# Delta-rule blocks: key transposes and key/query products issued one hook step later

## The chip, the cores and the metric

One core of a Trainium2 chip runs the whole program. The metric is the device time of one execution in microseconds (us); lower is better. In what follows TensorE does the matmuls and transposes (PE in the rows, PEld for its weight loads), VectorE is DVE, ScalarE is ACT, GpSimd is POOL, and SyncE (SP) issues nearly all DMAs.

## What is computed

One decoder layer over 2048 tokens of width 1024: an RMS norm, one combined input projection, two token mixers in parallel, a gated merge and an output projection. All of it is float32. Mixer A is a chunked gated delta rule with 4 heads of width 128 and a short causal convolution ahead of it; mixer B is dilated sliding-window attention. The part that matters here is the preparation of mixer A:

```python
qkv = jax.nn.silu(causal_depthwise_conv(dn_qkv, conv_w[layer]))      # width 4
dq, dk, dv = jnp.split(qkv.astype(jnp.float32), 3, axis=-1)
dq = l2_normalize(to_heads(dq)) * (HEAD_DIM ** -0.5)
dk = l2_normalize(to_heads(dk))
...
decay = jnp.exp(jnp.where(causal, gc[..., :, None] - gc[..., None, :], -jnp.inf))
lower = jnp.where(strict, jnp.einsum('bhnid,bhnjd->bhnij', kb, k) * decay, 0.0)
a_intra = jnp.where(causal, jnp.einsum('bhnid,bhnjd->bhnij', q, k) * decay, 0.0)
```

For every head the keys have to be convolved, gated, transposed and normed, and the products of keys with keys and of keys with queries have to be formed and multiplied with a decay matrix. Norms and signs are applied later as scales of rows.

## The kernel before, in words

The program has stages: attention (mixer B) with its projections; then the "channel units", in which TensorE multiplies 128 columns of the input weight with the normed input; inside them, as background work, the delta-rule preparation, an inverse and a scan; at the end the output. The change lies among the channel units.

`cunits` runs over the units. A unit has four blocks of 512 tokens (n = 0 to 3). A block is 24 matmuls into one accumulator `mm` (three buffers): for each of eight k, three products of high and low parts (L524 to L526). After every second k, thus after two groups of three matmuls, `hook()` is called; a block has four such hook steps, the last of them after its last matmul. When a block is done, the unit's own function is called with the accumulator, and it queues its later steps by `self.at(d, f)`: f is called in the d-th hook after that. The order in which the Python code issues instructions in this part is the order in which TensorE, VectorE, ScalarE and GpSimd execute them, since it is pinned for these four engines; the DMAs of SP are ordered by the scheduler. Steps that fall due in one hook are called by their tick and then by the length that the list of waiting steps had when they were queued.

For each of the four heads there is a unit of keys (`k_block`), one of queries (`q_block`) and one of values (`v_block`), twelve units in a row. All three start with `conv`: ScalarE evicts the accumulator into `xr` (L624), VectorE (or for values ScalarE, L630) scales it into `acc` (L628) and adds three shifted products (L632). Four hooks later the gate follows: tanh on ScalarE (L636) and a product on VectorE (L637), which gives `kT` or `qT`.

- Keys: `pe(0)` and `pe(2)` each transpose two 128x128 pieces of kT on TensorE into a buffer `tp` (L688; two buffers), and ScalarE reads each piece twice, for the sum of squares (L692) and scaled into `kd` (L693). `fin` makes the norms on GpSimd (L700 to L706).
- Queries: `prep(0)` and `prep(2)` split keys and queries into high and low parts, ScalarE writing `kqh` (L727) and GpSimd `kql` (L728; two buffers each). `pe(0)` and `pe(2)` transpose two pieces of qT (L737), form the products by three matmuls for each of two pieces (L741 to L743) into `sc`, ScalarE takes squares (L745) and VectorE multiplies with the decay matrix E (L746), which `pe(2)` then stores with four DMAs. `fin` makes the norms (L760 to L762).
- Values: `pe` transposes four pieces seven hooks after the block (L780, read by L783).

`e_chain` makes the decay matrices of a head, four blocks one after the other through a single buffer `gcb`: a DMA loads it (L651), GpSimd adds the causal mask (L655), VectorE makes four differences (L662) and ScalarE their exponentials (L669). For the first head it starts ahead of the first key unit, for each later head in the value unit of the head before. The weights of the next unit are loaded and split in the same steps (ScalarE L78, GpSimd L79).

Of the kernel before, what the change touches and what calls it, by code (L numbers as in the profile page):

```python
# [36 lines left out]
def dr(ap, off, dims):  # L37
    return bass.AP(tensor=ap.tensor, offset=ap.offset + off, ap=[list(d) for d in dims])


class Net:
# [634 lines left out]
    def k_block(self, h, n, pr):  # L676
        nc, dp = self.nc, self.dp
        if n == 0:
            self.kT = dp.tile([P, T], F32, name="kT", bufs=1)
        kT = self.kT[:, n * 512:(n + 1) * 512]  # L680
        self.conv(n, 4 + h, pr, kT, lambda: self.recput(n, h, R_KT, P, kT.rearrange("p (a c) -> p a c", c=P)))
        ss = dp.tile([P, 12], F32, name="ss", bufs=3)
        kd = dp.tile([P, 4, P], F32, name="st4", bufs=2)

        def pe(t0):
            pt = self.ps.tile([P, 512], F32, name="tp", bufs=2)
            for t in (t0, t0 + 1):
                nc.tensor.transpose(pt[:, (t - t0) * P:(t - t0 + 1) * P], kT[:, t * P:(t + 1) * P], self.ident)  # L688
            for t in (t0, t0 + 1):
                c = h * 16 + n * 4 + t  # L690
                a = pt[:, (t - t0) * P:(t - t0 + 1) * P]
                nc.scalar.activation(kd[:, t, :], a, AF.Square, accum_out=ss[:, t:t + 1])  # L692
                nc.scalar.activation(kd[:, t, :], a, AF.Identity, scale=self.ek[:, c:c + 1])  # L693
            if t0 == 2:
                self.recput(n, h, R_KD, P, kd)

        def fin():
            cs = slice(h * 16 + n * 4, h * 16 + n * 4 + 4)
            G = nc.gpsimd
            G.tensor_scalar(out=ss[:, 0:4], in0=ss[:, 0:4], scalar1=4 * EPS, scalar2=None, op0=ALU.add)  # L700
            G.tensor_tensor(out=ss[:, 4:8], in0=ss[:, 0:4], in1=self.mhalf[:, 0:4], op=ALU.pow)
            G.tensor_tensor(out=ss[:, 8:12], in0=ss[:, 4:8], in1=self.beta[:, cs], op=ALU.mult)
            G.tensor_scalar(out=self.vss[:, cs], in0=ss[:, 8:12], scalar1=0.5, scalar2=None, op0=ALU.mult)
            G.tensor_tensor(out=ss[:, 8:12], in0=ss[:, 8:12], in1=ss[:, 4:8], op=ALU.mult)
            G.tensor_scalar(out=self.nbr[:, cs], in0=ss[:, 8:12], scalar1=-1.0, scalar2=None, op0=ALU.mult)
            G.tensor_tensor(out=self.ksn[:, cs], in0=self.nbr[:, cs], in1=self.egc[:, cs], op=ALU.mult)  # L706
        self.at(7, lambda: pe(0))
        self.at(9, lambda: pe(2))
        self.at(11, fin)

    def q_block(self, h, n, pr):
        nc, dp = self.nc, self.dp
# [9 lines left out]
        def prep(t0):  # L722
            kqh = dp.tile([P, 2, 2, P], F32R, name="kqh", bufs=2)
            kql = dp.tile([P, 2, 2, P], F32R, name="kql", bufs=2)
            kq[t0] = kqh, kql
            for j, src in enumerate((kv, qv)):
                nc.scalar.activation(kqh[:, :, j, :], src[:, t0:t0 + 2, :], AF.Copy)  # L727
                nc.gpsimd.tensor_tensor(out=kql[:, :, j, :], in0=src[:, t0:t0 + 2, :], in1=kqh[:, :, j, :].bitcast(F32),  # L728
                                        op=ALU.subtract)

        def pe(t0):
            E = self.E[h, n]
            kqh, kql = kq[t0]
            pt = self.ps.tile([P, 512], F32, name="tp", bufs=2)
            pk = self.ps.tile([P, 512], F32, name="sc", bufs=2)
            for t in (t0, t0 + 1):
                nc.tensor.transpose(pt[:, (t - t0) * P:(t - t0 + 1) * P], qT[:, t * P:(t + 1) * P], self.ident)  # L737
            for j in (0, 1):
                b = pk[:, j * 256:j * 256 + 256]
                rh, rl = (a[:, j].rearrange("p a c -> p (a c)") for a in (kqh, kql))  # L740
                nc.tensor.matmul(b, kqh[:, j, 0, :], rh, start=True, stop=False)  # L741
                nc.tensor.matmul(b, kqh[:, j, 0, :], rl, start=False, stop=False)
                nc.tensor.matmul(b, kql[:, j, 0, :], rh, start=False, stop=True)  # L743
            for t in (t0, t0 + 1):
                nc.scalar.activation(sq, pt[:, (t - t0) * P:(t - t0 + 1) * P], AF.Square, accum_out=ss[:, t:t + 1])  # L745
            nc.vector.tensor_tensor(out=la[:, t0:t0 + 2], in0=pk.rearrange("p (a b c) -> p a b c", b=2, c=P),  # L746
                                    in1=E[:, t0:t0 + 2, :].unsqueeze(2).to_broadcast([P, 2, 2, P]),
                                    op=ALU.mult)
            if t0 == 2:
                lt = la[:, :, 0, :]  # L750
                self.recput(n, h, R_AT, P, la[:, :, 1, :])
                self.recput(n, h, R_LO, 64, lt[0:64, :, 64:128], 64)
                for s in (0, 1):
                    nc.sync.dma_start(dr(self.lscr, ((h * 16 + n * 4) * 2 + s) * 4096, [[64, 64], [8192, 4], [1, 64]]),
                                      lt[s * 64:(s + 1) * 64, :, s * 64:(s + 1) * 64])
# [6 lines left out]
            G.tensor_scalar(out=self.cq[:, cs], in0=ss[:, 4:8], scalar1=SCALE, scalar2=None, op0=ALU.mult)  # L762
        self.at(6, lambda: prep(0))
        self.at(7, lambda: prep(2))
        self.at(9, lambda: pe(0))
        self.at(10, lambda: pe(2))
        self.at(12, fin)

    def v_block(self, h, n, pr):
        nc, dp = self.nc, self.dp  # L770
# [446 lines left out]
```

## Time and profile before

| | |
|---|---|
| median of 3 runs | 2385.1 us (2384.5 to 2389.4) |
| the profiled execution | 2384.28 us |
| its span, first to last instruction | 2382.4 us |
| granted TensorE clock, mean | 0.996 |
| busy: TensorE / VectorE / ScalarE / GpSimd | 98% / 50% / 36% / 37% |
| the delta-rule units, four heads | about 1119 to 1441 us, some 80 us a head |

The profile is one execution. Busy shares are of the span. A row of the timeline gives the start, the length, the engine, the line, the operation, and in brackets the idle time ahead of it with what ended it. Starts are measured; the ends of matmuls are modelled, which is why a row of pipelined matmuls seems to overlap.

### The profile page before, as it was taken

The numbers are of one execution on the slowest core, as the hardware profiler recorded it, in microseconds if no ns is written. First come the engines' busy times: TensorE is split into PE (matmuls) and PEld (weight loads), VectorE is DVE, ScalarE is ACT, GpSimd is POOL, SyncE is SP. The second block draws the span as 40 slices with busy tenths as digits, with TensorE's granted clock in tenths as the row PEclk, the third lists the DMA queues.
The fourth block names the chain that finished last, engine by engine and source line by source line (L and its number), as shares of the span: only waits on it lengthen the run. The fifth ranks groups of instructions, "written<-read, shape, count | busy, mean of one in ns | idle before, by whom it ended". The sixth has DMA issues, their size and how long they took to land.

```text
span 2382.4 us, 40700 instructions
## 1 busy us (share of the span) xinstructions
PE 2343.1 (98%) x13640; PEld 2133.7 (90%) x13640; DVE 1191.4 (50%) x2831; ACT 847.5 (36%) x3021; POOL 886.0 (37%) x1855
## 2 busy tenths in 40 slices
PE   8999999999999999999999999999999999999999
PEld 7899999999999999988878888888888878889988
DVE  5543344334334434344877775999344433454431
ACT  6433333344444434333666662111233313111110
POOL 6633333333333334310855671101233212433441
PEclk9999999999999999999999999999999999999999
DMA  8443344333333335233544443222577645554542
GB/s 283 158 116 111 107 123 121 95 103 112 110 97 112 108 91 128 86 91 92 142 121 130 116 115 116 69 73 75 193 209 203 182 151 157 164 178 156 149 140 75
DMA packets 378808, 307.30 MB, mean 129 GB/s; under 512 B 61352, under 2 KB 345320, under 8 KB 378216
## 3 DMA queue, kind: packets, MB, share of 16 engines
q1 hardware_dynamic: 378312, 304.64, 43.6%
q8 instruction: 108, 1.77, 0.3%
q14 instruction: 100, 0.82, 0.1%
q10 hardware_dynamic: 288, 0.07, 0.0%
HBM read 187.92 MB, written 116.69 MB: 128 GB/s over the span
## 4 chain that ended last, share of the span: by engine, by line
PE 85%; POOL 4%; DMA 4%; DVE 4%; ACT 2%; issue 2%; SPq 0%; POOLq 0%; ACTq 0%; DVEq 0%
PE mm L240 10%; PE mm L238 10%; PE mm L239 10%; PE mm L524 9%; PE mm L526 9%; PE mm L525 9%; PE mm L1054 2%; PE mm L1052 2%; PE mm L1053 2%; PE mm L1035 2%; PE mm L1037 2%; PE mm L1036 2%; PE po L333 2%; PE tp L290 2%; DMA gcb<-gcscr 1%
## 5 line engine op out<-in xcount | busy, mean ns | idle before, releaser
L238 PE MATMUL mm<-wh,hh 128*128 128x384 f32 (+1 forms) x1536 | 555.0, 361 | 6.3 <-ACT hh L131 2.9
L240 PE MATMUL mm<-wh,hl 128*128 128x384 f32 (+1 forms) x1536 | 519.7, 338 | 1.7 <-DVE hl L135 1.7
L239 PE MATMUL mm<-wl,hh 128*128 128x384 f32 (+1 forms) x1536 | 518.3, 337 | 0.7 <-DVE wl L79 0.6
L524 PE MATMUL mm<-hh,wh 128*128 128x512 f32 x1152 | 464.1, 403 | 0.0
L526 PE MATMUL mm<-hh,wl 128*128 128x512 f32 x1152 | 454.7, 395 | 0.0
L525 PE MATMUL mm<-hl,wh 128*128 128x512 f32 x1152 | 451.4, 392 | 0.0
L238 PEld LDWEIGHTS mm<-wh,hh 128*128 128x128 f32 x1536 | 290.2, 189 | 10.8 <-ACT wh L78 4.4
L239 PEld LDWEIGHTS mm<-wl,hh 128*128 128x128 f32 x1536 | 291.0, 189 | 1.7 <-DVE wl L79 1.1
L240 PEld LDWEIGHTS mm<-wh,hl 128*128 128x128 f32 x1536 | 289.3, 188 | 2.6 <-DVE hl L135 2.6
L526 PEld LDWEIGHTS mm<-hh,wl 128*128 128x128 f32 x1152 | 217.0, 188 | 46.9
L525 PEld LDWEIGHTS mm<-hl,wh 128*128 128x128 f32 x1152 | 217.4, 189 | 41.8
L524 PEld LDWEIGHTS mm<-hh,wh 128*128 128x128 f32 x1152 | 217.2, 189 | 42.0
L263 DVE SCALAR_TENSOR_TENSOR rec<-mm,st,wqk 128x128 f32<-128x128 f32 x384 | 116.7, 346 | 263.7 <-POOL st L255 244.2
L79 POOL TENSOR_TENSOR wl<-raw,wh 128x512 fp32r<-128x512 f32 (+1 forms) x73 | 104.6, 1445 | 382.3 <-ACT wh L78 382.0
L317 ACT ACTIVATE p<-sc,ol 128x128 f32<-128x128 f32 (+1 forms) x192 | 82.1, 428 | 316.8 <-DVE ol L315 273.0
L253 POOL TENSOR_SCALAR st<-st 128x2 f32<-128x2 f32 x192 | 38.0, 198 | 399.7 <-ACT rec L249 398.2
L249 ACT ACTIVATE rec<-mm 128x128 f32<-128x128 f32 x384 | 102.7, 273 | 185.0 <-PE mm L240 171.8
L1035 PE MATMUL mm<-oh,hh 128*128 128x256 f32 x512 | 143.9, 281 | 2.9 <-DVE gt L1039 2.9
L1037 PE MATMUL mm<-oh,hl 128*128 128x256 f32 x512 | 142.9, 279 | 0.0
L1036 PE MATMUL mm<-ol,hh 128*128 128x256 f32 x512 | 142.9, 279 | 0.0
L255 POOL TENSOR_TENSOR st<-st,mhalf 128x2 f32<-128x2 f32 x192 | 135.0, 703 | 16.0
L632 DVE SCALAR_TENSOR_TENSOR acc<-xr,cw,acc 128x512 f32<-128x512 f32 x144 | 122.4, 850 | 17.4 <-ACT acc L630 12.4
(244 smaller groups left out, 4332.0 us busy)
## 6 DMA issues: line engine op xcount, KB each, us to landing
rscr<-rec SPq DMA_DIRECT2D x192, 192.0 KB, 1.9
raw<-in_w_in_dram SPq DMA_DIRECT2D x138, 256.0 KB, 3.1
qk<-rscr SPq DMA_DIRECT2D x192, 128.0 KB, 2.2
gscr<-gt SPq DMA_DIRECT2D x64, 256.0 KB, 2.4
gt<-gscr SPq DMA_DIRECT2D x64, 256.0 KB, 3.5
oscr<-ol SPq DMA_DIRECT2D x192, 65.0 KB, 2.0
oc<-oscr SPq DMA_DIRECT2D x16, 780.0 KB, 5.3
v<-rscr SPq DMA_DIRECT2D x192, 64.0 KB, 2.0
```

The lines of the kernel that those rows point to most:

```text
L238: nc.tensor.matmul(pr[:, :w], a, wh[:, k, :w], start=(k == 0), stop=False)
L239: nc.tensor.matmul(pr[:, :w], a, wl[:, k, :w], start=False, stop=False)
L240: nc.tensor.matmul(pr[:, :w], b, wh[:, k, :w], start=False, stop=(k == KT - 1))
L255: nc.gpsimd.tensor_tensor(out=st[:, 2:4], in0=st[:, 0:2], in1=self.mhalf[:, 0:2], op=ALU.pow)
L263: nc.vector.scalar_tensor_tensor(out=qk[:, j, :], in0=pr[:, j * P:(j + 1) * P], scalar=st[:, 2 + j:3 + j], in1=s["w"][2][:, j, :], op0=ALU ...
L524: nc.tensor.matmul(pr, wh[:, k, :], a, start=(k == 0), stop=False)
L525: nc.tensor.matmul(pr, wh[:, k, :], b, start=False, stop=False)
L526: nc.tensor.matmul(pr, wl[:, k, :], a, start=False, stop=(k == KT - 1))
L632: nc.vector.scalar_tensor_tensor(out=acc, in0=xr[:, j:j + 512], scalar=w[:, j:j + 1], in1=acc, op0=ALU.mult, op1=ALU.add)
L1035: nc.tensor.matmul(o, self.wbh[:, k, ms], oh[:, k, :], start=(k == b * 4), stop=False)
L1036: nc.tensor.matmul(o, self.wbh[:, k, ms], ol[:, k, :], start=False, stop=False)
L1037: nc.tensor.matmul(o, self.wbl[:, k, ms], oh[:, k, :], start=False, stop=(k == b * 4 + 3))
```

## The change

In `k_block` the two pairs of transposes and the step `fin` are queued for one hook later (7, 9, 11 become 8, 10, 12). In `q_block` the two groups of transposes and products and `fin` are queued one hook later too (9, 10, 12 become 10, 11, 13); `prep` stays at 6 and 7. Nothing else is changed, and no instruction is added or taken away.

```diff
 def k_block(self, h, n, pr):
...
-        self.at(7, lambda: pe(0))
-        self.at(9, lambda: pe(2))
-        self.at(11, fin)
+        self.at(8, lambda: pe(0))
+        self.at(10, lambda: pe(2))
+        self.at(12, fin)
...
 def q_block(self, h, n, pr):
...
         self.at(6, lambda: prep(0))
         self.at(7, lambda: prep(2))
-        self.at(9, lambda: pe(0))
-        self.at(10, lambda: pe(2))
-        self.at(12, fin)
+        self.at(10, lambda: pe(0))
+        self.at(11, lambda: pe(2))
+        self.at(13, fin)
```

On TensorE, in the second head's key unit, the first pair of key transposes before (mm_15320 is the accumulator of the unit's third block, mm_15371 of its fourth):

```order
L688 MATMUL tp_15343<-ident_69,kT_15243 128x128 x2
L524 MATMUL mm_15320<-hh_67,wh1_14955 128x512
L525 MATMUL mm_15320<-hl_68,wh1_14955 128x512
L526 MATMUL mm_15320<-hh_67,wl1_14956 128x512
...
L524 MATMUL mm_15371<-hh_67,wh1_14955 128x512
```

and after the change:

```order
L525 MATMUL mm_15320<-hl_68,wh1_14952 128x512
L526 MATMUL mm_15320<-hh_67,wl1_14953 128x512
L688 MATMUL tp_15352<-ident_69,kT_15243 128x128 x2
L524 MATMUL mm_15371<-hh_67,wh1_14952 128x512
L525 MATMUL mm_15371<-hl_68,wh1_14952 128x512
```

The pair stood before the last six matmuls of a block; now it stands between two blocks. On ScalarE, at the same pair, the order before (kT from acc is the tanh of the next block's gate, L78 the split of a weight, L624 an eviction):

```order
L669 ACTIVATE E_15300<-E_15300,nlc_13338 128x128 x4
L692 ACTIVATE st4_15253,ss_15252<-tp_15343 128x128
L693 ACTIVATE st4_15253<-tp_15343,ek_13340 128x128
...
L636 ACTIVATE kT_15243<-acc_15313 128x512
L78 ACTIVATE wh1_15254<-raw_15258 128x512
L624 ACTIVATE xr_15361<-mm_15320 128x512
```

and now:

```order
L669 ACTIVATE E_15300<-E_15300,nlc_13338 128x128 x4
L636 ACTIVATE kT_15243<-acc_15313 128x512
L692 ACTIVATE st4_15253,ss_15252<-tp_15352 128x128
L693 ACTIVATE st4_15253<-tp_15352,ek_13340 128x128
...
L78 ACTIVATE wh1_15254<-raw_15258 128x512
L624 ACTIVATE xr_15361<-mm_15320 128x512
```

The gate of the next block now precedes the four reads of the pair. On ScalarE in the second head's query unit, around the first block's two groups (sq are the squares of the queries, kqh the high parts for the second block), a piece of the difference:

```order
 L624 ACTIVATE xr_15621<-mm_15563 128x512
-L745 ACTIVATE sq_15491,ss_15490<-tp_15639 128x128 x2
-L745 ACTIVATE sq_15491,ss_15490<-tp_15658 128x128 x2
-L727 ACTIVATE kqh_15675<-kT_15243 128x2x128
-L727 ACTIVATE kqh_15675<-qT_15551 128x2x128
+L745 ACTIVATE sq_15491,ss_15490<-tp_15645 128x128 x2
+L727 ACTIVATE kqh_15658<-kT_15243 128x2x128
+L727 ACTIVATE kqh_15658<-qT_15551 128x2x128
+L745 ACTIVATE sq_15491,ss_15490<-tp_15670 128x128 x2
 L727 ACTIVATE kqh_15687<-kT_15243 128x2x128
 L727 ACTIVATE kqh_15687<-qT_15551 128x2x128
```

The copies for the first half of the second block moved between the squares of the first block's two groups.

## Rows read from the trace of the kernel before

**Rows 1.** The page, part 1: busy time in us, share of the span and number of instructions of each engine.

```profile
PE 2343.1 (98%) x13640; PEld 2133.7 (90%) x13640; DVE 1191.4 (50%) x2831; ACT 847.5 (36%) x3021; POOL 886.0 (37%) x1855
```

**Rows 2.** Busy time by stretch, the delta-rule units of heads one to four: the stretch, its length, then busy us and instructions of TensorE, its weight loads, VectorE, ScalarE and GpSimd, the granted clock, the share of the DMA engines and GB/s.

```profile
1119.00:1200.00 81.00, 79.30 (x391) 65.39 (x390) 64.64 (x100) 51.16 (x167) 53.65 (x69) 1.00 0.53 135
1200.00:1281.00 81.00, 78.65 (x390) 64.89 (x389) 61.40 (x96) 50.00 (x164) 49.80 (x67) 1.00 0.47 123
1281.00:1361.00 80.00, 78.73 (x391) 65.07 (x390) 61.78 (x96) 50.19 (x165) 49.12 (x66) 1.00 0.46 122
1361.00:1441.00 80.00, 78.78 (x394) 65.13 (x392) 57.93 (x80) 46.24 (x151) 47.08 (x64) 1.00 0.42 109
```

**Rows 3.** Who waited for whom, TensorE alone, 1100 to 1460 us: total us, times, longest.

```profile
PE tp L688 <- DVE kT L637: 5.4, 4, 2.1
PE sc L742 <- POOL kql L728: 0.8, 3, 0.3
```

**Rows 4.** Timeline of TensorE in the second head: an undisturbed key pair with the group of matmuls before it and the matmul after, and an undisturbed query group with the matmul after it.

```profile
1225.46 0.39 PE L524 MATMUL mm<-hh,wh 128*128 128x512 f32 x1
...
1226.15 0.38 PE L688 MATMUL tp<-ident,kT 128*128 128x128 f32 x2
1226.29 0.47 PE L524 MATMUL mm<-hh,wh 128*128 128x512 f32 x1
...
1237.82 0.38 PE L737 MATMUL tp<-ident,qT 128*128 128x128 f32 x2
...
1238.75 0.39 PE L524 MATMUL mm<-hh,wh 128*128 128x512 f32 x1
```

**Rows 5.** Timeline of TensorE: the late key pair of each head, each behind the start of the last group of matmuls before it.

```profile
1134.88 0.39 PE L524 MATMUL mm<-hh,wh 128*128 128x512 f32 x1
...
1137.11 0.44 PE L688 MATMUL tp<-ident,kT 128*128 128x128 f32 x2 [1.37 <-DVE kT L637]
...
1208.28 0.39 PE L524 MATMUL mm<-hh,wh 128*128 128x512 f32 x1
...
1211.21 0.44 PE L688 MATMUL tp<-ident,kT 128*128 128x128 f32 x2 [2.08 <-DVE kT L637]
...
1288.29 0.39 PE L524 MATMUL mm<-hh,wh 128*128 128x512 f32 x1
...
1290.15 0.44 PE L688 MATMUL tp<-ident,kT 128*128 128x128 f32 x2 [1.00 <-DVE kT L637]
...
1367.10 0.39 PE L524 MATMUL mm<-hh,wh 128*128 128x512 f32 x1
...
1368.91 0.44 PE L688 MATMUL tp<-ident,kT 128*128 128x128 f32 x2 [0.95 <-DVE kT L637]
```

**Rows 6.** Timeline of TensorE: the late query group of each head, from its first transpose to the next matmul.

```profile
1165.14 0.38 PE L737 MATMUL tp<-ident,qT 128*128 128x128 f32 x2
...
1166.64 0.40 PE L524 MATMUL mm<-hh,wh 128*128 128x512 f32 x1
...
1245.18 0.38 PE L737 MATMUL tp<-ident,qT 128*128 128x128 f32 x2
...
1246.65 0.40 PE L524 MATMUL mm<-hh,wh 128*128 128x512 f32 x1
...
1324.12 0.38 PE L737 MATMUL tp<-ident,qT 128*128 128x128 f32 x2
...
1325.58 0.39 PE L524 MATMUL mm<-hh,wh 128*128 128x512 f32 x1
...
1402.87 0.38 PE L737 MATMUL tp<-ident,qT 128*128 128x128 f32 x2
...
1404.33 0.39 PE L524 MATMUL mm<-hh,wh 128*128 128x512 f32 x1
```

**Rows 7.** Timeline of VectorE, SP's queue and GpSimd in the second head's chain to kT: an undisturbed set of four differences, then the load of the last decay block, its mask, the weight split beside it, the differences and the product that completes kT.

```profile
1192.65 1.13 DVE L662 SCALAR_TENSOR_TENSOR E<-gcb,ngc 128x128 f32<-128x128 f32 x4
...
1202.00 8.98 SPq L651 DMA_DIRECT2D gcb<-gcscr  x2
...
1207.09 1.29 POOL L655 TENSOR_TENSOR gcb<-gcb,cmask 128x512 f32<-128x512 f32 x1 [6.34 <-DMA gcb<-gcscr]
1208.34 1.28 POOL L79 TENSOR_TENSOR wl<-raw,wh 128x512 fp32r<-128x512 f32 x1
...
1208.41 2.14 DVE L662 SCALAR_TENSOR_TENSOR E<-gcb,ngc 128x128 f32<-128x128 f32 x4 [2.85 <-POOL gcb L655]
1210.48 0.68 DVE L637 SCALAR_TENSOR_TENSOR kT<-kT,acc 128x512 f32<-128x512 f32 x1
```

**Rows 8.** The queries of the second head: busy time from 1240 to 1260 us (columns as in rows 2), then from the timeline ScalarE's first copy for the second block and GpSimd's first subtraction for it.

```profile
1240.00:1260.00 20.00, 19.73 (x106) 16.56 (x105) 16.65 (x22) 12.17 (x41) 19.08 (x26) 1.00 0.48 118
...
1241.27 0.41 ACT L727 ACTIVATE kqh<-kT 128x256 fp32r<-128x256 f32 x1
...
1244.02 1.19 POOL L728 TENSOR_TENSOR kql<-kT,kqh 128x256 fp32r<-128x256 f32 x1
```

**Rows 9.** Timeline of ScalarE in the second head: the gate behind the first key pair, and the first and last read of the second pair.

```profile
1214.29 0.63 ACT L636 ACTIVATE kT<-acc 128x512 f32<-128x512 f32 x1 [1.12 <-DVE acc L632]
...
1215.82 0.27 ACT L692 ACTIVATE st<-tp 128x128 f32<-128x128 f32 x1
...
1216.87 0.37 ACT L693 ACTIVATE st<-tp,ek 128x128 f32<-128x128 f32 x1
```

## The prediction

> **What bounds the kernel now.** I read the busy shares first, then the four head stretches of the delta-rule part, then who made TensorE wait there, and last the timeline around each such wait. TensorE is busy 98% of the span [rows 1], so time goes away only where it stands still. In the stretch that the change touches, TensorE is busy 79.30 of 81, 78.65 of 81, 78.73 of 80 and 78.78 of 80 us, at a granted clock of 1.00 (the 2.4 GHz level) throughout; VectorE and GpSimd have 16 to 33 us of slack per head [rows 2]. The idle 6.5 us have few causes: 5.4 us in four waits of the key transposes (L688) for kT and 0.8 us in three waits of the products (L742) for kql [rows 3]; in the first head a query group is late as well [rows 6]. All of them are at instructions that the change moves.
>
> What one wait really costs I take from starts, since ends of matmuls are modelled. Undisturbed, the last group of three matmuls before a pair of key transposes starts 0.69 us ahead of them, and the next matmul follows the pair after 0.14 us; a query group (two transposes, six products) takes 0.93 us from its start to the next matmul [rows 4]. Against that, the four late key pairs start 2.23, 2.93, 1.86 and 1.81 us after their last group [rows 5]: 1.54, 2.24, 1.17 and 1.12 us lost. To each goes some 0.06 us, since a pair that waited takes 0.44 us in place of 0.38 [rows 4, 5]: 1.6, 2.3, 1.2, 1.2, together 6.3 us. The four late query groups take 1.50, 1.47, 1.46 and 1.46 us in place of 0.93 [rows 6]: 0.57, 0.54, 0.53, 0.53, together 2.2 us. So 8.5 us is all that the change can win here.
>
> **The change part by part.** It adds and removes no instruction. One hook step is two groups of three matmuls: by the 0.69 us of a group [rows 4] that is 1.37 us of TensorE work put ahead of every key pair and every query group.
>
> *Key pairs.* The late kT has nothing to do with TensorE's pace at that moment. In the second head the mask of decay block 3 is loaded at 1202.00, GpSimd adds it at 1207.09, VectorE makes the difference from 1208.41 for 2.14 us, and only behind that, in VectorE's order, comes the product that completes kT, from 1210.48 [rows 7]. TensorE's pair starts at 1211.21. None of these instructions is moved: VectorE's order is the same in both kernels. With 1.37 us of matmuls ahead of the pair, the waits lose min(1.37, cost): 1.37 + 1.37 + 1.2 + 1.2 = 5.1 us, leaving about 0.2 us in the first head and 0.9 us in the second. Ends: 6.3 us if the chain also comes earlier; less if it comes later by what a disturbed difference costs. That price has rows: the same four differences take 1.13 us alone and 2.14 us with the weight split L79 beside them [rows 7], so 1.0 us; on top in two of the four heads it leaves 3.1 us, in all four some 1.1 to 1.5. I take 5.1, since the chain's own instructions keep their order.
>
> On that collision the Trainium skill, GPSIMD Engine Reference, section 1. Specifications, says that GpSimd shares its SBUF interfaces with VectorE and contends with VectorE instructions that have two SBUF inputs. The differences and L632 are such instructions, and the rows agree with it. By that rule the new place of L79, which now runs ahead of three small GpSimd operations at each passage from queries to values, would slow L632 in place of a difference and leave the sum at 5.1 us, or slow a difference and make it 3.1.
>
> *Query groups.* These wait for kql, which GpSimd makes one after the other: at 1240 to 1260 it is busy 19.08 of 20 us, and kql of the second block starts at 1244.02 although its kqh was there from 1241.27 on [rows 8]. If GpSimd's queue stays where it is and TensorE's group comes 1.37 us later, a loss of 0.55 goes entirely. But the key waits saved ahead of it bring TensorE forward again by 1.37, 1.37, 1.2 and 1.2 us within each head, so in absolute time the group stands where it was; what then decides is whether GpSimd is earlier. ScalarE's new order issues the first kqh of the queries ahead of the last key pair's squares (1.4 us of ScalarE work, 1215.82 to 1217.24 in rows 9), and the gate ahead of the pair before. In heads two to four that brings GpSimd forward by an estimated 0.5 to 1.1 us (the 1.4 less what its own queue swallows), enough for the 0.54, 0.53 and 0.53 us: 1.6 us gained. In the first head ScalarE is held up by the decay chain's exponentials as well, and the split L78 that GpSimd waits for gets behind a group of squares: I book 0.5 us of loss there (between 0 and the 1.4 of such a group; less than half, as the two delays overlap with GpSimd's own queue). Ends for all four: +2.2 and, if none is earlier and one is later, -1.4.
>
> *Reads of the transposes (ScalarE).* From the second head on each first key pair's squares now stand behind the gate of the next block, and the gate waits for VectorE: 1.12 us in the row shown, to 1214.29 [rows 9]. Queued behind that wait are the squares, the eviction L624 and so VectorE's next convolution; who may wait for it is TensorE, for one of the two tp buffers. The pair of 1211.21 would be read from 1214.9 (the gate takes 0.63) to 1216.3, and its buffer is wanted again two pairs on, eight groups and two pairs later, 5.8 us, at 1217.0: a margin of 0.7 us. I book nothing; if the cover is gone, TensorE waits for the excess once per block.
>
> A rule that speaks against this edit: the Trainium skill, PSUM — Partial Sum Buffer, section Engine vs sequencer instructions, says that ScalarE's queue is strict first-in first-out, so the squares cannot pass the waiting gate. Rows 9 agree (the second pair's squares start only after the gate and the eviction). By the rule alone each of twelve pairs is at risk; by the margin none is, and the sum stays.
>
> *Queries against values.* The last query group of each head now stands directly ahead of (in the last head: right behind) the first value transposes, which need the tp buffer of the group before. That one was issued 2.3 us earlier (0.93 + 1.37), and ScalarE's two squares are half of the 1.4 us that a key pair's reads take: no wait. GpSimd's fin chains and SP's stores of la shift behind the two splits or by a hook; nothing on TensorE reads cq before the scan. Free.
>
> **Sum.** 5.1 + 1.6 - 0.5 = 6.2 us off the profiled execution, whose own time is 2384.3 us for a span of 2382.4. That gives 2378.1 us. The three runs shown have a median of 2385.1, so the profiled one lies 0.8 under it; I put the forecast at 2378.3. After the delta-rule part TensorE is still the bound, and its later waits depend on hooks, which come earlier with it, so I let the whole 6.2 us reach the end.
>
> **The rivals.**
> *The late data stays late (about no change).* The differences collide with L79 anew, keys win only 3.1 us, and the query waits stay as they are because TensorE was brought forward by as much as it was put back: 2384.3 - 3.1 = 2381.2 us. For it: the chain to kT is timed by loads of about 5 us, not by the edit [rows 7]; against it: every load in it begins with an instruction that follows TensorE. It is also where the case ends in which the gain is lost again by a later wait for a transfer (2384 us); nothing in the 98% speaks for that.
> *GpSimd starves among the queries (slower).* kqh has two buffers, and the copies for the next block now stand in the same step as the group that still reads the old ones; before, the first of them had a step between. If each of two copies in three block changes per head starts later by a whole group (0.93 us), GpSimd stands still for 5.6 us per head. It has 0.92 in 20 to spare [rows 8], about 1.2 in a query stretch (a third of a head's 80 us), so its kql would be 4.4 us late at the end; less the 1.37 by which the group itself is later, TensorE waits 3.0 us per head, 12 us in all, less the 5.1 of the keys: 2391 us. It decides the sign once GpSimd loses more than some 2.6 us per head. Against it: kqh lay ready 2.3 us before GpSimd reached it [rows 8], more than the step of 1.37.
> *It doesn't do what it says* is excluded by the order: every key pair and query group does stand six matmuls later.
>
> **How the numbers follow.** Forecast 0.60, late data 0.25, lost again later 0.07, starving 0.08. A measurement of this kernel tells about 0.2% apart, 4.8 us; the forecast is beyond it, near enough that a little of its chance would fall inside, and some of the late-data case outside, which I let cancel and lean by 0.02: faster 0.62, same 0.30, slower 0.08. The range goes from all 8.5 us won (2375.6) to the late-data case with half of its gain lost (2383): it leaves out the starving case and most of the loss later on.
>
> **What would show it.** Right: L688's waits in TensorE's list fall from 5.4 to about 1 us, with one of 0.7 to 1.0 us left in the second head at 1210 or so; L742's go to at most one, in the first head; ScalarE's waits on TensorE before the query squares become waits of kqh for the products. The four head stretches shorten by about 1.4, 1.9, 1.7 and 1.7 us, and the first by less for its query group. Wrong: a TensorE wait on ScalarE's squares for a tp buffer (the margin of 0.7 us), GpSimd idle among the kql, or a difference L662 of 2.1 us that was 1.1 before; and a span that shrinks by less than the sum of the four stretches would show the gain given back later.

## The result, and the profile after

| | median us | range | runs |
|---|---|---|---|
| before | 2386.18 | 2383.57 to 2389.40 | 11 |
| after | 2391.92 | 2388.87 to 2395.35 | 11 |

The ratio is 1.0025, with a 95% interval of 1.0017 to 1.0034: the change makes the kernel slower by some 5.7 us, where a gain of 6.8 us had been forecast. The profiled execution of after took 2393.3 us for a span of 2391.5, so it lies 1.4 us above its median.

Who TensorE waited for in the changed kernel, 1100 to 1480 us: total us, times, longest.

```profile
PE sc L742 <- POOL kql L728: 7.2, 5, 1.8
PE tp L688 <- DVE kT L637: 3.7, 4, 1.1
PE tp L780 <- DVE xr L620: 2.3, 3, 0.9
```

Against [rows 3], the waits of the key transposes fell, though by 1.7 us and not by 5; the products' waits grew from 0.8 to 7.2, and value transposes now wait too. With 0.3 us at L741, before had 6.5 us in all; now it is 13.2.

The four head stretches of after, columns as in rows 2:

```profile
1119.00:1200.00 81.00, 78.35 (x379) 64.46 (x378) 62.64 (x96) 48.38 (x163) 55.68 (x68) 0.98 0.49 128
1200.00:1281.00 81.00, 77.77 (x386) 64.06 (x385) 60.06 (x93) 48.38 (x164) 53.82 (x66) 1.00 0.46 120
1281.00:1361.00 80.00, 76.38 (x378) 62.90 (x377) 60.37 (x92) 47.12 (x160) 53.80 (x66) 1.00 0.45 120
1361.00:1441.00 80.00, 76.30 (x379) 62.81 (x378) 57.33 (x86) 47.64 (x158) 49.84 (x65) 1.00 0.43 112
```

TensorE is busy 0.9 to 2.5 us less in each of the four windows than in [rows 2], so every head loses. The granted clock of the first is 0.98 where it was 1.00.

TensorE in the second head of after, in order of time: the first key pair, a key pair later in the unit, the late query group, and the late value transposes and key pair at the end of the head.

```profile
1214.29 0.44 PE L688 MATMUL tp<-ident,kT 128*128 128x128 f32 x2 [0.95 <-DVE kT L637]
...
1229.25 0.38 PE L688 MATMUL tp<-ident,kT 128*128 128x128 f32 x2
...
1235.19 0.38 PE L688 MATMUL tp<-ident,kT 128*128 128x128 f32 x2
...
1250.43 0.39 PE L742 MATMUL sc<-kql,kqh 128*128 128x256 f32 x1 [1.65 <-POOL kql L728]
...
1287.00 0.66 PE L780 MATMUL tp<-ident,qT 128*128 128x128 f32 x4 [0.82 <-DVE xr L620]
...
1295.66 0.44 PE L688 MATMUL tp<-ident,kT 128*128 128x128 f32 x2 [1.12 <-DVE kT L637]
```

The pair at 1214.29 left 0.95 us where 0.9 was forecast; the next head's still waits 1.12, about as long as before [rows 5]. In the query unit one wait of 1.65 us replaces a loss of half a microsecond [rows 6]. The releaser named for L780 is only the last VectorE instruction seen; what the transposes read is the gated value (the rows call its tile qT too), whose product L637 runs from 1286.27 for 0.68 us.

**What makes the products late.** Timeline of ScalarE, then of VectorE, in the key unit of that head: one block's gate, the first and last read of the key pair, the eviction, the next gate; and VectorE's first step of four convolutions.

```profile
1223.50 0.63 ACT L636 ACTIVATE kT<-acc 128x512 f32<-128x512 f32 x1 [1.87 <-DVE acc L632]
1224.04 0.26 ACT L692 ACTIVATE st<-tp 128x128 f32<-128x128 f32 x1
...
1225.08 0.37 ACT L693 ACTIVATE st<-tp,ek 128x128 f32<-128x128 f32 x1
1225.35 0.59 ACT L624 ACTIVATE xr<-mm 128x512 f32<-128x512 f32 x1
...
1229.11 0.63 ACT L636 ACTIVATE kT<-acc 128x512 f32<-128x512 f32 x1 [1.86 <-DVE acc L632]
```

```profile
1220.36 0.75 DVE L628 TENSOR_SCALAR acc<-mm,cw 128x512 f32<-128x512 f32 x1 [1.56 <-ACT xr L624]
...
1225.97 0.75 DVE L628 TENSOR_SCALAR acc<-mm,cw 128x512 f32<-128x512 f32 x1 [1.03 <-ACT xr L624]
...
1231.58 0.75 DVE L628 TENSOR_SCALAR acc<-mm,cw 128x512 f32<-128x512 f32 x1 [1.10 <-ACT xr L624]
...
1237.71 0.75 DVE L628 TENSOR_SCALAR acc<-mm,cw 128x512 f32<-128x512 f32 x1 [1.55 <-ACT xr L624]
```

The four reads of the moved pair, 1.4 us, stand between gate and eviction. VectorE's L628 reads the same accumulator as the eviction, and starts 0.03 us after the eviction's end (1225.35 + 0.59, then 1225.97); its row names the eviction as what it waited for. (The Trainium skill, PSUM — Partial Sum Buffer, PSUM bank collisions raise a hardware error, says that two engines must not access one bank in the same 32 partitions at the same time; the rows agree.) Then come L632 and the next gate. So ScalarE and VectorE go round in a loop of 5.61 us (1223.50 to 1229.11). TensorE goes through a block in 5.94 us (1229.25 to 1235.19). The loop starts late in each head, since the late kT starts it, and gains only 0.33 us on TensorE per block. VectorE's own list of waits, 1100 to 1480 us, sums it up; before, the same line had 2.0 us in two waits:

```profile
DVE acc L628 <- ACT xr L624: 21.0, 19, 1.7
```

At the end of the key unit stands the weight split, ScalarE's L78 and with it GpSimd's L79. Timeline of GpSimd at the passage to the queries, first in before:

```profile
1232.14 1.31 POOL L79 TENSOR_TENSOR wl<-raw,wh 128x512 fp32r<-128x512 f32 x1 [1.20 <-ACT wh L78]
...
1234.33 1.19 POOL L728 TENSOR_TENSOR kql<-kT,kqh 128x256 fp32r<-128x256 f32 x1 [0.88 <-ACT kqh L727]
```

and in after:

```profile
1237.27 1.31 POOL L79 TENSOR_TENSOR wl<-raw,wh 128x512 fp32r<-128x512 f32 x1 [0.54 <-ACT wh L78]
1238.53 0.74 POOL L728 TENSOR_TENSOR kql<-kT,kqh 128x256 fp32r<-128x256 f32 x1
...
1248.52 1.17 POOL L728 TENSOR_TENSOR kql<-kT,kqh 128x256 fp32r<-128x256 f32 x1
```

The split starts 5.1 us later and the first block's subtraction 4.2 us later. The second block's subtraction, at 1244.02 in [rows 8], is now at 1248.52: 4.5 us later. TensorE's group that needs it starts at 1248.27, against 1245.18 in [rows 6]: 3.1 us later, the moved hook included. So GpSimd has lost 1.4 us on the group, and that is nearly all of the 1.65 us of wait. From 1240 to 1260 GpSimd is busy 19.16 us (19.08 in [rows 8]): it doesn't starve, it started late. The copies kqh that it reads are a different matter: ScalarE now waits with them for the products, 30.6 us in 16 waits between 1100 and 1480 us, where before it was 1.4 us in three:

```profile
ACT kqh L727 <- PE sc L743: 30.6, 16, 3.4
```

What that costs shows in the experiments.

**And the clock.** In the first head, with one wait of 1.78 us, the granted clock leaves the upper level for a while. Windows of 5 us, columns as in rows 2:

```profile
1160.00:1165.00 5.00, 5.00 (x27) 4.23 (x26) 4.59 (x9) 4.30 (x17) 4.50 (x8) 1.00 0.49 143
1165.00:1170.00 5.00, 3.22 (x16) 2.56 (x15) 4.93 (x6) 1.60 (x6) 5.00 (x6) 0.84 0.63 156
1170.00:1175.00 5.00, 5.00 (x24) 4.15 (x23) 2.53 (x5) 2.54 (x11) 4.75 (x7) 0.82 0.36 99
```

The parts that were not granted add up to (0.16 + 0.18) x 5 = 1.7 us. Waits 6.7 us longer and 1.7 us for the clock make 8.4 of the 9.1 us by which the spans of the two profiled executions differ.

### The profile page after: what moved, and what is told of

Its sections match the earlier page's. It is cut to its first block, busy times and chain, and to the rows that moved or that the text cites. A ratio compares the mean times of both kernels' runs of the same rounds, so it can differ in the third digit from the quotient of the medians.

```text
span 2391.5 us, 40680 instructions
## 1 busy us (share of the span) xinstructions
PE 2345.8 (98%) x13640; PEld 2134.1 (89%) x13640; DVE 1189.8 (50%) x2831; ACT 843.1 (35%) x3021; POOL 901.8 (38%) x1855
## 4 chain that ended last, share of the span: by engine, by line
PE 83%; POOL 6%; DVE 4%; DMA 3%; ACT 2%; issue 2%; SPq 0%; POOLq 0%; DVEq 0%; ACTq 0%
PE mm L238 10%; PE mm L240 10%; PE mm L239 10%; PE mm L524 8%; PE mm L526 8%; PE mm L525 8%; PE mm L1052 2%; PE mm L1054 2%; PE mm L1053 2%; PE mm L1035 2%; PE mm L1037 2%; PE mm L1036 2%; PE po L333 2%; PE tp L290 2%; DMA gcb<-gcscr 1%
## 5 line engine op out<-in xcount | busy, mean ns | idle before, releaser
L79 POOL TENSOR_TENSOR wl<-raw,wh 128x512 fp32r<-128x512 f32 (+1 forms) x73 | 106.0, 1464 | 385.6 <-ACT wh L78 385.6
L632 DVE SCALAR_TENSOR_TENSOR acc<-xr,cw,acc 128x512 f32<-128x512 f32 x144 | 128.1, 890 | 9.7 <-ACT acc L630 3.9
```

The lines of the kernel that those rows point to most:

```text
L632: nc.vector.scalar_tensor_tensor(out=acc, in0=xr[:, j:j + 512], scalar=w[:, j:j + 1], in1=acc, op0=ALU.mult, op1=ALU.add)
```

## The experiments

I set out with three theories of the slowdown. **A**: the moved key pair's reads lengthen the loop of ScalarE and VectorE as just read, and GpSimd starts late. **B**, the prediction's slower rival: the copies kqh, behind the moved query groups, starve GpSimd. **C**: on GpSimd the weight split now runs ahead of the queries' norms, and that delays the decay chain. **D** came after the second run: ScalarE's copies wait for the moved products and hold back the gates behind them, so the next head's differences come late. Waits are TensorE's in the one profiled execution, 1100 to 1480 us; L741's go with the products. A stretch at a lower clock is one in which the granted clock of 5 us windows falls below 0.99 there. The profiled execution lies between 4.1 us under (e5) and 3.2 us above (e8) the median of its run, so waits and medians can be set against each other only to within some us.

| run | keys | products | values | stretches at a lower clock | median us | its before | ratio, 95% interval |
|---|---|---|---|---|---|---|---|
| before | 5.4 | 1.1 | 0 | 0 | | | |
| after | 3.7 | 7.2 | 2.3 | 1 | 2391.9 | 2386.2 | 1.0017 to 1.0034 |
| e1 | 0.6 | 10.6 | 0 | 2 | 2393.5 | 2385.3 | 1.0020 to 1.0045 |
| e2 | 8.9 | 0 | 1.4 | 2 | 2392.7 | 2385.3 | 1.0019 to 1.0039 |
| e3 | 3.6 | 1.5 | 2.1 | 0 | 2386.5 | 2385.3 | 0.9997 to 1.0014 |
| e5 | 3.2 | 6.2 | 2.5 | 0 | 2391.1 | 2385.3 | 1.0013 to 1.0031 |
| e6 | 8.9 | 1.2 | 1.9 | 3 | 2396.6 | 2385.7 | 1.0034 to 1.0060 |
| e7 | 0.2 | 2.9 | 0 | 0 | 2382.5 | 2385.7 | 0.9979 to 0.9997 |
| e8 | 3.0 | 1.5 | 0.9 | 0 | 2383.0 | 2385.7 | 0.9983 to 1.0000 |
| e9 | 3.5 | 0.4 | 4.3 | 0 | 2387.5 | 2385.7 | 1.0003 to 1.0020 |
| e10 | 8.2 | 0 | 0 | 2 | 2387.2 | 2385.6 | 0.9996 to 1.0014 |
| e11 | 2.8 | 2.5 | 0 | 0 | 2382.9 | 2385.6 | 0.9976 to 0.9994 |
| e12 | 1.8 | 1.5 | 0.3 | 0 | 2382.8 | 2385.6 | 0.9975 to 0.9993 |
| e13 | 6.9 | 0 | 0 | 1 | 2385.8 | 2386.4 | 0.9987 to 1.0005 |

### Each half alone (e1, e2)

e1 takes the queries' hooks back to 9, 10, 12; e2 the keys' to 7, 9, 11.

```diff
 # e1, q_block, against after
-        self.at(10, lambda: pe(0))
-        self.at(11, lambda: pe(2))
-        self.at(13, fin)
+        self.at(9, lambda: pe(0))
+        self.at(10, lambda: pe(2))
+        self.at(12, fin)
```

> Only the key pairs and their norms one step later, queries as before. Theory A (the squares of a key pair now stand on ScalarE between the gate and the eviction, the loop of VectorE and ScalarE in the key unit gets longer, and GpSimd's work for the queries starts 2 us later): the query groups are a step earlier against the same late GpSimd, so the waits of the products rise from 7.2 to 11 to 13 us, and the time is at or above that of the whole change, 2391 to 2397 us. Theory B (the copies kqh behind the moved query groups starve GpSimd): the products' waits fall to 2 us or less, 2381 to 2383 us. Theory C (the weight split ahead of the query norms delays the decay chain, which keeps key and value waits): GpSimd's order at the passage to the values is as before, the value waits of 2.3 us are gone.

> Only the query groups and their norms one step later, keys as before. A: the products' waits are gone (0 to 0.5 us), key waits 5.4 us as before, 2384 us. B: the products wait 7 us or more, 2391 us and above. C: value waits of 2 us and key waits above 5.4 us, up to 2390 us, without waits of the products.

With the keys alone, key waits are nearly gone (0.6) and the products wait 10.6, close to what A expected. B falls, for no query group has moved. With the queries alone the products don't wait at all, which is against B once more. But the time is 2392.7 and not 2384: the key waits, of instructions that e2 doesn't move, grow from 5.4 to 8.9. Each half alone costs 8.2 and 7.4 us, where both together cost 5.7; the intervals overlap, so all that is shown is that the costs don't add up. A doesn't explain e2. Its waits (1.4 us at values, 8.9 at keys) are rather what C expected, which e5 tests below; D is the other explanation.

### The reads behind the eviction (e3)

```diff
-                fn(n, pr)
+                fn(n, pr); [f() for f in self.post.pop(self.tick, [])]
...
-        self.at(8, lambda: pe(0))
+        self.post.setdefault(self.tick + 8, []).append(lambda: pe(0))
```

> The whole change, but each first key pair is issued after the eviction of the block that ends there, so that ScalarE's order is gate, eviction, reads. TensorE's, VectorE's and GpSimd's orders are those of the change. A: the products' waits fall from 7.2 to 2 us or less, 2384 to 2387 us. B: they stay at 7 us, 2392 us. C alone: the same as the change, value waits of 2 us.

Timeline of ScalarE in e3, second head: gate, eviction, first read, and the next two gates.

```profile
1221.16 0.63 ACT L636 ACTIVATE kT<-acc 128x512 f32<-128x512 f32 x1 [1.34 <-DVE acc L632]
1221.70 0.58 ACT L624 ACTIVATE xr<-mm 128x512 f32<-128x512 f32 x1
1222.18 0.27 ACT L692 ACTIVATE st<-tp 128x128 f32<-128x128 f32 x1
...
1225.65 0.63 ACT L636 ACTIVATE kT<-acc 128x512 f32<-128x512 f32 x1 [0.74 <-DVE acc L632]
...
1230.09 0.63 ACT L636 ACTIVATE qT<-acc 128x512 f32<-128x512 f32 x1 [0.70 <-DVE acc L632]
```

The loop takes 4.49 and 4.44 us in place of 5.61, so it gains some 1.5 us on TensorE's 5.94 per block, and VectorE's waits at L628 fall from 21.0 to 2.9 us. GpSimd's first subtraction for the second block, at 1248.52 in after, is back at 1243.91:

```profile
1243.91 0.74 POOL L728 TENSOR_TENSOR kql<-kT,kqh 128x256 fp32r<-128x256 f32 x1
```

The products' waits fall from 7.2 to 1.5, with the orders of TensorE and GpSimd unchanged. That shows A for the products, and 4.5 of the 5.7 us (each against its own before; the two intervals don't overlap). What stays is 3.6 us at keys and 2.1 at values.

### GpSimd's norms where they were (e5)

```diff
 # k_block, q_block, against after
-        self.at(12, fin)
+        self.at(11, fin)
...
-        self.at(13, fin)
+        self.at(12, fin)
```

> The whole change except the two norm steps, which stay at 11 and 12, so that GpSimd's order is word for word that of the kernel before. C: value waits gone, key waits 1.5 us or less, 2387 us; the products still wait 7 us. A or B alone: like the change, 2391 to 2393 us, value and key waits as there.

The waits for keys and values stay (3.2 and 2.5 us), although GpSimd has its old order, so C falls. (The products' waits fall by 1 us; the time can't be told apart from after's.)

### The gates ahead of the copies (e6, e10)

Both are e2 with gates taken out from behind the copies: e6 those of the queries, e10 the one of the first value block alone.

```diff
 # e6, conv
-        self.at(4, gate)
+        self.at(4, gate) if ct >= 4 else self.ev.append((self.tick + 3, -1, gate))
 # e10, conv
-        self.at(4, gate)
+        self.at(4, gate) if ct < 8 or n else self.ev.append((self.tick + 3, -1, gate))
```

> The kernel with the queries alone moved, and in it the gate (L636) and its product (L637) of a query block stand ahead of the squares and copies of the group before it instead of behind them; the orders of TensorE and GpSimd do not differ from the kernel with the queries alone moved, which had 8.9 us of waits for transposes of keys (L688), 1.4 us for transposes of values (L780), none for products, and took 2392.7 us. Theory D (ScalarE's copies L727 wait for the moved products, hold the gate back behind them, and so VectorE's convolutions and the decay differences come later): the waits for keys fall to 4 to 6.5 us and those for values to 0.5 us or less, 2384 to 2388 us. Rival (the lateness comes from TensorE's or GpSimd's own order, which stays): the waits for keys stay at 8 to 10 us, 2391 to 2395 us.

> The queries alone moved, with the gate of the first value block (and its product on VectorE) put one hook step earlier and ahead of the second half of the copies and squares; the orders of TensorE and GpSimd stay. The run with the gates of the queries put ahead left that gate behind the copies, at the same distance, and its waits for keys stayed at 8.9 us. Theory D, narrowed (the copies that wait for the moved products hold back the gate of the first value block, and with it the four differences of the next head): the gate comes some 2 us earlier, the differences 1 to 1.5 us, the waits for keys fall from 8.9 to 4 to 6 us, no dip of the granted clock is left, 2383 to 2388 us. Rival (VectorE's differences wait for something on GpSimd or TensorE): the waits for keys stay at 8 to 10 us, 2390 to 2395 us.

e6 was a miss: the key waits stayed at 8.9 us, as its rival had it, and the time rose to 2396.6; what made it slower than e2 was not followed. So the gates of the queries are not what D needs. The trace names another one: the gate ahead of the differences is that of the first value block, which e6 leaves behind the copies. e10 moves that one. In e2 the timeline of ScalarE has those copies and that gate, and of VectorE and TensorE the first set of differences and the first value transposes (the releaser cq of the first row is a small GpSimd step; in after the same wait of 2.09 us is put down to the products):

```profile
1256.62 0.42 ACT L727 ACTIVATE kqh<-kT 128x256 fp32r<-128x256 f32 x1 [2.09 <-POOL cq L762]
...
1258.92 0.42 ACT L727 ACTIVATE kqh<-kT 128x256 fp32r<-128x256 f32 x1 [0.93 <-PE sc L743]
...
1260.20 0.62 ACT L636 ACTIVATE qT<-acc 128x512 f32<-128x512 f32 x1
...
1266.19 1.14 DVE L662 SCALAR_TENSOR_TENSOR E<-gcb,ngc 128x128 f32<-128x128 f32 x4
...
1266.02 0.60 PE L780 MATMUL tp<-ident,qT 128*128 128x128 f32 x4
```

and e10 at the same place:

```profile
1256.12 0.42 ACT L727 ACTIVATE kqh<-kT 128x256 fp32r<-128x256 f32 x1 [2.09 <-POOL cq L762]
...
1257.70 0.63 ACT L636 ACTIVATE qT<-acc 128x512 f32<-128x512 f32 x1 [0.21 <-issue]
...
1261.36 3.30 DVE L632 SCALAR_TENSOR_TENSOR acc<-xr,cw,acc 128x512 f32<-128x512 f32 x3 [1.63 <-ACT acc L630]
...
1261.57 1.75 POOL L79 TENSOR_TENSOR wl<-raw,wh 128x512 fp32r<-128x512 f32 x1
...
1264.58 1.13 DVE L662 SCALAR_TENSOR_TENSOR E<-gcb,ngc 128x128 f32<-128x128 f32 x4
...
1265.52 0.60 PE L780 MATMUL tp<-ident,qT 128*128 128x128 f32 x4
```

Counted from the first copy, the gate comes at 1.58 us instead of 3.58. Counted from the value transposes, the differences come 0.94 us ahead instead of 0.17 behind. The time against its own before falls from 7.4 us in e2 to 1.6 in e10, by 5.8 us, and the two intervals don't overlap; nothing is moved on TensorE or GpSimd. So the place of this one gate on ScalarE (its product on VectorE goes with it) costs that time, which is D; but the waits did not fall as D said, and for the keys they lie in the rival's range. Values went from 1.4 to 0, keys only from 8.9 to 8.2, and two stretches at a lower clock remain in the profiled execution (2388.7 us, 1.4 above its median). One reason stands in the rows: the convolution ahead of the differences begins earlier, but takes 3.30 us, where the same three L632 took 2.33 in e2 and 2.40 in before. GpSimd's mask and split, which they had run all but clear of, are now beside them.

### The rest of the copies out of the way (e13)

```diff
 # q_block, against e10
-        self.at(7, lambda: prep(2))
+        self.at(7, lambda: prep(2)) if n < 3 else self.post.setdefault(self.tick + 8, []).append(lambda: prep(2))
```

> The queries alone moved, with the gate of the first value block ahead as in the run before (8.2 us of waits for keys, the differences 1.1 us earlier instead of 2), and in the fourth query block the second half of the copies behind the eviction and the next gate's product instead of ahead of them, so that they hold back neither; on GpSimd the mask and the weight split then stand ahead of that half's subtractions, the orders of TensorE and VectorE stay. Theory D in full (ScalarE's copies hold back gate and eviction, and both set the next head's differences): the waits for keys fall to 3 to 6 us, products 1 us or less, 2382 to 2386 us. Rival (the rest of the waits for keys has nothing to do with ScalarE's copies): they stay at 7 to 9 us, 2386 to 2390 us.

The keys wait 6.9 us, above the 3 to 6 expected and a little under the rival's 7 to 9, so this run doesn't decide between the two; the time, 2385.8, is no different from before. The convolution starts earlier once more, but still takes 3.25 us, now beside the end of the split and the last subtractions. Where the first differences stand against the first value transposes, in the second head, and what the third head's first key pair then waits:

| | differences | transposes | lead | key wait | key pair at hook |
|---|---|---|---|---|---|
| before | 1262.87 | 1265.17 | 2.30 | 1.00 | 7 |
| e13 | 1263.98 | 1265.07 | 1.09 | 1.43 | 7 |
| e10 | 1264.58 | 1265.52 | 0.94 | 1.61 | 7 |
| e2 | 1266.19 | 1266.02 | -0.17 | 2.22 | 7 |
| e12 | 1262.09 | 1263.04 | 0.95 | 0.34 | 8 |
| after | 1268.74 | 1268.16 | -0.58 | 1.12 | 8 |

Among the runs with the same hook the key wait follows the lead, by about half of it: 2.47 us of lead lost from before to e2 are 1.22 us of wait. Of the rest, 0.73 us is taken up on the way: from these differences to the key pair it is 27.28 us in before and 26.55 in e2.

In the whole change a collision adds to the late gate. The three L632 directly ahead of these differences, in before:

```profile
1260.55 2.40 DVE L632 SCALAR_TENSOR_TENSOR acc<-xr,cw,acc 128x512 f32<-128x512 f32 x3 [0.95 <-ACT acc L630]
```

and in after:

```profile
1264.65 4.17 DVE L632 SCALAR_TENSOR_TENSOR acc<-xr,cw,acc 128x512 f32<-128x512 f32 x3
```

Before, they start 4.62 us ahead of the value transposes; in after, 3.51. That is 1.1 of the 2.9 us of lead lost. The other 1.8 us is their length: GpSimd's mask (1264.48) and split (1265.73) run beside them. The third head is alike (3.53 us ahead, 4.17 long in after). In the first head they start 2.5 us later against the transposes but take 2.33, as before, with no collision.

### Only the keys, and the whole change, mended (e7, e8, e11, e9, e12)

e7 is e1 with e3's edit; e8 and e11 put the norms of the fourth key block eight and four hooks later on top (with six buffers ss). e9 is after with e3's, e6's and e8's edits; e12 is after with e3's and e10's.

```diff
 # e8 (in e11: 16), k_block
-        self.at(12, fin)
+        self.at(12 if n < 3 else 20, fin)
```

> The keys alone moved (as in the first run, with 10.6 us of waits for products and 0.6 us for keys), with the reads of the first pair of each key block put behind the eviction on ScalarE. Theory A (the reads between gate and eviction lengthen the loop of VectorE and ScalarE, and GpSimd starts late): the waits for products fall to 1 to 5 us, the waits for keys stay at 3.5 us or less, 2382 to 2387 us. Rival (the later place on TensorE itself costs it): the waits for products stay at 9 us or more, 2391 to 2395 us.

> As the run before it in this list, and the norms of the fourth key block (seven small GpSimd instructions, some 4.5 us beside the products) are put eight hooks later, behind the subtractions of the third query block. If GpSimd's queue is what the products wait for (theory A's last step), their waits fall to 1 us or less with the waits for keys as there, 2379 to 2384 us, below the kernel before. If the products wait for something else (ScalarE's copies, or the gate of the queries), their waits stay as in that run and the time too.

> The keys alone moved with the reads behind the eviction (2382.5 us, 2.9 us of waits for products, both long ones in the first head), and the norms of the fourth key block four hooks later instead of eight. If the norms stand ahead of the subtractions that the first head's products wait for: waits for products 1.5 us or less, for keys 1 us or less, 2380 to 2382.5 us. Rival (the norms push the masks and so the differences, as with eight hooks): waits for keys 2 to 3 us come back and the time is 2383 us or more.

> The whole change, with the reads of the first key pair behind the eviction, the gates of the queries ahead of the moved groups' squares and copies, and the norms of the fourth key block eight hooks later. Theories A and D together: waits for products 1 us or less, for keys 1 to 3.5 us, for values 1 us or less, 2379 to 2384 us. If something else than these two makes the change slow, waits of 6 us or more in all remain, 2386 us or more.

> The whole change, with two orders on ScalarE put right: the reads of the first key pair behind the eviction, the gate of the first value block ahead of the second half of the copies. With the first alone the waits were 1.5 us (products), 3.6 (keys) and 2.1 (values), 2386.5 us. Theories A and D together: keys 2.5 us or less, values 1 us or less, products 2 us or less, 2381 to 2385 us. Rival (only the first order matters): waits and time as with the first alone, 2385 to 2388 us.

TensorE's longest waits in e7, and then in e12 (views as for after):

```profile
PE sc L742 <- POOL kql L728: 2.9, 4, 1.5
```

```profile
PE tp L688 <- DVE kT L637: 1.8, 3, 0.9
PE sc L742 <- POOL kql L728: 1.5, 1, 1.5
```

e7 confirms A for the keys alone: ScalarE's order takes the products' waits from 10.6 to 2.9 us, and 11.4 us of time. Both e7 and e12 are faster than before by 3 us (0.12% and 0.16%; both intervals stay below 1), and so faster than after too. e12 is the whole change with two orders on ScalarE put right, and TensorE and GpSimd have the order of after; so those two account for all of the slowdown. The second of them is worth some 4 us beyond e3 (each against its own before). e8 and e11 were misses: against e7 the late norms take 1.4 and 0.4 us from the products' waits, but the keys wait 2.8 and 2.6 us more, and there is no gain over e7 that can be told. e9 was a miss: products 0.4 as expected, but 4.3 us at values and 3.5 at keys. It carries e6's gates, which did not help there, and e8's late norms; which of the two makes the values late I did not separate.

## Why the prediction was wrong

- **Reads of the transposes: the step that failed.** The prediction named the eviction and VectorE's next convolution as queued behind the late gate, then asked only who on TensorE waits for a tp buffer, and booked nothing. The tp buffers never made TensorE wait. The waiter was VectorE's L628, 1.0 to 1.6 us per key block, and behind it the split and GpSimd. Putting the reads behind the eviction takes that price away: 4.5 us in e3, with the keys alone 11.4 us in e7. None of the three waits or lengths that were to show a wrong forecast appeared: TensorE does not wait for the squares, GpSimd's waits for kqh fall from 2.7 to 1.7 us, and no set of differences that took 1.1 us takes 2.1. They all watched for other mechanisms. A margin in the buffer was worked out; the round trip gate, reads, eviction, convolution, gate was not, though the durations for it were at hand: the loop grows by most of the 1.4 us of the reads in [rows 9] (from some 4.5 us in e3 to 5.61), and has to be set against TensorE's block. The rule of the Trainium skill that the prediction weighed there (PSUM — Partial Sum Buffer, Engine vs sequencer instructions: ScalarE's queue is first-in first-out) was the one to follow, not to its buffer but to its next instruction; the reads from 1224.04 and the eviction at 1225.35 show it at work.
- **Query groups, 1.6 gained less 0.5.** This rested on GpSimd coming 0.5 to 1.1 us earlier, by the order of the first kqh. GpSimd came later instead (first subtraction of the second block by 4.5 us), and 6.1 us of waits were lost. The premise that GpSimd's late queue decides these waits held: it is busy 19.16 of 20 us there.
- **Key pairs, 5.1.** The order argument held in e1, where nothing else delays the chain: 5.4 us of waits became 0.6. In the whole change only 1.7 us of waits were gained. The first differences stand 2.9 us later there against the value transposes (table above), and e12, with the orders of TensorE and GpSimd of after but both orders on ScalarE put right, has 1.8 us of key waits in place of after's 3.7. "The chain's own instructions keep their order" is true and not enough: VectorE's convolution ahead of them comes behind ScalarE's gate, and that stood behind copies that wait for the moved products. The collision that I had put the price on (differences beside L79, 2.14 us in [rows 7]) stayed as it was, 2.17 us at 1292.83 in after. The prediction also let L79 slow L632 and left the sum at 5.1 us. That was wrong, for L632 stands ahead of the differences in VectorE's order: slowed to 4.17 us in after, it pushes them back. In e10 too it is the convolution that collides (3.30 against 2.33 us), as the Trainium skill has it for VectorE instructions with two SBUF inputs beside GpSimd (GPSIMD Engine Reference, section 1. Specifications).
- **Queries against values: free.** They cost 2.3 us of waits. In the rows the product that completes the values stands on VectorE directly behind a set of differences (1285.21 for 1.14 us, then 1286.27), which are late for the same reason; e10 and e12, with the gate ahead, wait 0 and 0.3 us there.
- **The slower rival.** Its place was right (the copies issued in the same step as the group that reads the old buffers) but its mechanism wrong. ScalarE did wait there for the products (2.09 and 0.93 us), but GpSimd waited for the copies less than before (1.7 us against 2.7). With the queries alone it does wait 7.0 us for them, and TensorE waits for no product. The damage went through the gate behind the copies. e12 keeps 24.8 us of these waits and is faster than before, so they cost nothing by themselves. The estimate of 2391 was near the 2391.9 by accident.
- **The clock** was not in the sum. Each stretch of lower clock cost 1.7 us.
- **The shortening should reach the end** held in e7, with 3.4 us less of waits and 3.2 us less of time, and in e12, with 2.9 us of each.
- **Two slips of arithmetic** changed nothing: 8.5 us off 2384.3 is 2375.8 and not 2375.6, and 6.2 us off the two bases is 2378.1 and 2378.9, not 2378.3.

What stays open: in e10 and e13 the key waits fell less than expected while the time fell by 5.8 us and more. The longer convolution accounts for some 0.9 us per head of what the gate gave; the rest may be the scatter of single executions, from which the waits are taken; that was not settled.

## What to carry to other kernels

When a step moves back in an in-order queue, ask what now stands behind it that used to be ahead, and follow each of those to the engine that feeds the queue's next wait; if the path closes into a loop, compare its period with the pace of the bounding engine: here a loop faster by 0.33 us per block did not make up its late start within the unit. Price copies into double buffers as waits of the engine that makes the copy, with everything queued behind them, not only as starvation of the engine that reads it. And issue what closes the loop (gate, eviction) ahead of what only consumes (squares, scaled copies): here that alone turned 5.7 us lost into 3 us gained (e12).

## What I had not expected of the hardware

A short wait can cost more than itself. TensorE in e2 before and after a wait of 2.22 us:

```profile
1290.13 0.40 PE L526 MATMUL mm<-hh,wl 128*128 128x512 f32 x1
1292.74 0.53 PE L688 MATMUL tp<-ident,kT 128*128 128x128 f32 x2 [2.22 <-DVE kT L637]
...
1294.36 0.63 PE L524 MATMUL mm<-hh,wh 128*128 128x512 f32 x1
1294.78 0.63 PE L525 MATMUL mm<-hl,wh 128*128 128x512 f32 x1
...
1296.67 0.40 PE L524 MATMUL mm<-hh,wh 128*128 128x512 f32 x1
1296.91 0.40 PE L525 MATMUL mm<-hl,wh 128*128 128x512 f32 x1
```

For some 3 us the matmuls start 0.42 us apart and not 0.24: the 1.2 GHz level and not the 2.4 one. The windows there (granted 0.80 and 0.86 over 5 us each) give 1.7 us lost. The same followed the waits of 2.27 and 2.30 us in e1, 2.60 in e2, 2.37, 2.37 and 2.52 in e6, 2.42 and 2.41 in e10 and 2.29 in e13, but also that of 1.78 us in after; it did not follow one of 2.08 us in before [rows 5], one of 2.55 in e2, nor one of 2.29 in e1. So the length of the wait alone does not decide it.
